# Weights laid out by tiles, and the decode's gate sums taken for all samples in one product

## The chip, the core and the metric

The kernel runs on one core of one Trainium2 chip. The metric is the device time of one execution in microseconds (us), and lower is better. The kernel is built by hand from single instructions for the engines of the core: TensorE (PE, matrix products, with a separate record for its weight loads, PEld), VectorE (DVE), ScalarE (ACT), GpSimd (POOL) and SyncE (SP). SP, POOL and ACT also issue DMAs, and each of them has a queue of its own for that: the profile calls SP's queue q1, ACT's q10 and POOL's q0.

## What is computed

One inference step of a one-layer decoder in float32. A prompt of 1024 rows and 8 samples of one row each share the weights. Per layer:

```python
q, k, v, logf, u, z = mixer_inputs(rmsnorm(x), w_in, b_f, g_sgu_v)      # x @ w_in, columns split
...
c = cumsum(lf_all, axis=1)                  # forget gates, past positions from the paged cache, then the new one
s = q @ k_all.T * 64 ** -0.5 + (c[query] - c[key])
att = softmax(s) @ v_all                    # 8 heads of 64; a sample has 8192 past positions in 64 pages
x = x + concat(rmsnorm(att), rmsnorm(sgu(u, z))) @ w_o
x = x + cross_attend(rmsnorm(x), memory keys and values from w_ck, w_cv, with w_cq, w_co)
x = x + (silu(conv(gate)) * conv(val)) @ w_down      # h = rmsnorm(x) @ w_up
```

A sample's keys, values and gate logs are gathered from three caches through a page table: 16 gathers of 1 MB for the keys of a sample (4 positions by 512 numbers for each of 128 partitions), 16 for the values, and one of 256 KB for the gate logs (64 positions by 8 heads for each partition). A position's gate is the sum of all gate logs behind it. On the chip this is a scan inside each partition's 64 positions, and a product with a constant matrix of suffix sums, `suf`, over the 128 partitions' totals.

## The kernel before

The prompt sets the program: the input projection in the order of its columns q (O_Q), forget and u (O_F, 520 columns), k (O_K), v (O_V), z (O_Z), then attention in two halves, the output projection, cross attention and the MLP. Every float32 product is made of three products of split operands: a weight is loaded raw into `wr` (L249), ACT rounds it to `wh` (L235), DVE takes the rest `wl = wr - wh` (L236), and PE multiplies three times (L272 wh by u, L273 wl by u, L274 wh by the rest of u). So no product of L273 can start before DVE has made the `wl` of its pair of row blocks. `wr` and `wl` have 4 buffers each, `wh` 5, so that the splits of a stage also wait for the products of the stage before. A load brings 512 KB (256 rows by 512 columns), issued by SP in program order, so that all of SP's transfers stand in one line in q1. `wpair` (L264) gives the address of such a load.

Beside the prompt runs the decode of the 8 samples, as a background program that is stepped between pieces of the prompt's work (L1525 and on). For sample b it takes 16 steps ch: a gather of keys (POOL, L1428), a product with the query on DVE (L1444, or L1435 in attention) and a sum over the 64 numbers of each head (L1448 or L1436). The query is fetched by SP through a copy in memory (L1398). At ch 11 `gates_scan` gathers the gate logs (L1404), reorders them on ACT (L1407) and scans them on DVE (L1408). At ch 13 `gates` adds the 64th value of the scan to the new row's gate (L1413), multiplies with `suf` on PE (L1418, into the PSUM bank "ms", of which there is one, shared with the attention's products) and subtracts the scan on DVE (L1420), which gives `dec`. Then the values are gathered (L1489) and multiplied on PE (L1495).

All order is fixed when the program is built: each engine runs its rows in the order in which they were written, with `behind(...)` and `issue_after(...)` moving rows to a place behind what has been written on that engine, and waits only on semaphores. The names below: `kv` is a buffer of gathered keys or values (4 of them), `d` a buffer of 128x512 (5 of them, for queries, gate logs and scans), `s` a sample's scores, `lps` the sums of its exponentials, `fl` the prompt's forget logits, `lse` and `lf` the steps of their log sigmoid (L364 to L367).

Of the kernel before, what the change touches and what calls it, by code (L numbers as in the profile page):

```python
# [11 lines left out]
AF = mybir.ActivationFunctionType  # L12
ALU = mybir.AluOpType
# [5 lines left out]
P = 128  # L19
# [59 lines left out]
def build(nc, tc, ctx, a, phases=None):  # L79
# [27 lines left out]
    def nm(s):  # L107
        cnt[0] += 1
        return f"{s}_{cnt[0]}"
# [245 lines left out]
    lfz = const.tile([P, 64], F32, tag="lfz", name="lfz")  # L355
    lps = const.tile([P, 8, 8], F32, tag="lps", name="lps")
    dec = lambda tag: dpool.tile([P, 512], F32, tag=tag, bufs=1, name=nm(tag))
    vsum = dec("vsum").rearrange("p (b d) -> p b d", d=64)
# [15 lines left out]
    def p1(early):  # L374
# [13 lines left out]
        def load_x(kk, hf):  # L388

            raw = WRAW(1024).rearrange("p (k t) -> p k t", t=512)  # L390
            c = slice(hf * 512, hf * 512 + 512)
# [291 lines left out]
    def pmem():  # L683
# [9 lines left out]
        for q in range(2):  # L693
            h, l = U([P, 4, 256], F32R), U([P, 4, 256], F32R)
            raw = WRAW(1024).rearrange("p (k m) -> p k m", m=256)
            nc.sync.dma_start(raw, a["memT"][q * 512 : (q + 1) * 512, :].rearrange("(k p) m -> p k m", p=P))
            for k in range(4):
# [440 lines left out]
    def cross(xt, sq):  # L1138
# [84 lines left out]
        for n in range(2):  # L1223
            if n:
                ws = [wload(wpair(a["w_cq"], kk, n * 512, 512), 1024) for kk in range(4)]
            for dt_ in range(4):
# [35 lines left out]
        ys = []  # L1262
        sq = yield from out_proj(a["w_co"], oh, ol, xt, ys=ys)
        return ys
# [4 lines left out]
    def ffn(hf, xt, ys, late=None):  # L1269
# [21 lines left out]
        for gi, gn in enumerate(GROUPS):  # L1291
# [32 lines left out]
            for n in range(2):  # L1324
                ws = []
                for k2 in range(0, gn, 2):
                    m = min(2, gn - k2)
                    r0 = (f0 + k2) * P
                    h, l, _ = wload(
                        a["w_down"][r0 : r0 + m * P, n * 512 : (n + 1) * 512].rearrange("(k p) n -> p k n", p=P), m * 512  # L1330
                    )
                    for q in range(m):
                        ws.append((h[:, q, :], l[:, q, :]))
# [40 lines left out]
    def decode():  # L1374
# [35 lines left out]

        def gates(b, A):
            tot = sm([P, 8], "tot", 2)
            nc.vector.tensor_tensor(  # L1413
                tot, A.rearrange("p (h k) -> p h k", k=64)[:, :, 63], lfz[:, b * 8 : b * 8 + 8], op=ALU.add
            )
            ps = MS()
            with behind(ENG.PE):
                mmul(ps[:, :8], suf, tot, start=True, stop=True)  # L1418
            dt_ = dec("dec").rearrange("p (k h) -> p k h", h=8)
            nc.vector.tensor_tensor(  # L1420
                dt_, ps[:, :8].unsqueeze(1).broadcast_to((P, 64, 8)), A.rearrange("p (h k) -> p k h", k=64), op=ALU.subtract
            )
            return dt_
# [103 lines left out]
        for g in range(8 * 16 + 16 + VLAG + 2):  # L1527
# [326 lines left out]
    def prompt():  # L1854
# [38 lines left out]
        for hf in range(2):  # L1893
# [8 lines left out]
            if ends:  # L1902
                yield from ends.pop()
            sq = yield from out_proj(a["w_o"], mh, ml, xt, partial(load_x, hf))
            if hf == 0:
# [43 lines left out]
    "cpack", "gpack", "b_f", "g_sgu_v", "ws00", "bs00", "wsT", "w_in", "w_o", "w_cq", "w_ck", "w_cv", "w_co",  # L1949
    "w_up", "w_down", "g_final",  # L1950
]
# [6 lines left out]
def layout(np, i):  # L1958
# [15 lines left out]
    for m in range(2):  # L1974
# [8 lines left out]
        axis=1,  # L1983
    )
    x = n["x_prompt"][0]
    xs = n["x_sample"][:, 0]
    return {
        "x": f(x), "xT": f(x.T), "xs": f(xs), "xsT": f(xs.T.reshape(8, P, 8).transpose(1, 0, 2)),
        "cache_k": f(n["cache_k"]).reshape(-1, 4 * AW), "cache_v": f(n["cache_v"]).reshape(-1, 4 * AW),
        "cache_logf": f(n["cache_logf"]).reshape(-1, 64 * NH),  # L1990
        "cmk": f(n["cache_mem_k"][0]).reshape(NB, NMEM, D), "cmv": f(n["cache_mem_v"][0]).reshape(NB, NMEM, D),
        "stT": f(n["state_conv"][0].transpose(2, 1, 0).reshape(2 * NF, P, 16).transpose(1, 0, 2)),
        "pt": f(n["page_table"].T), "mem": f(n["mem_prompt"][0]), "memT": f(n["mem_prompt"][0].T),
        "cpack": cp, "gpack": f(gp), "b_f": f(n["b_f"]), "g_sgu_v": f(n["g_sgu_v"]),
        "ws00": f(n["w_s"][0][:, 0, 0][None]), "bs00": f(n["b_s"][0][:, 0][None]),
        "wsT": f(n["w_s"][0].transpose(2, 0, 1)),
        "w_in": f(n["w_in"][0]), "w_o": f(n["w_o"][0]), "w_cq": f(n["w_cq"][0]), "w_ck": f(n["w_ck"][0]),
        "w_cv": f(n["w_cv"][0]), "w_co": f(n["w_co"][0]),
        "w_up": f(n["w_up"][0].reshape(8, P, 2 * NF, P).transpose(2, 1, 0, 3)).reshape(2 * NF, P, D),
        "w_down": f(n["w_down"][0]), "g_final": f(n["g_final"][None]),  # L2000
    }
# [33 lines left out]
```

## Time and profile before

| what | before |
|---|---|
| time of three runs, us | 1790.99, 1791.04, 1794.76 (median 1791.04) |
| span of the profiled execution, us | 1791.7 |
| DVE busy, us | 1399.9 (78%) in 1733 instructions |
| ACT busy, us | 733.5 (41%) |
| POOL busy, us | 488.3 (27%) |
| DMA moved | 521.06 MB in 157074 packets |
| of it on q1 (SP) | 165.73 MB in 92874 packets |
| of it on q0 (POOL) | 341.14 MB in 57168 packets |

The profile has one execution, whose span is 1791.7 us; this is 0.7 us above the median of the runs. An engine's busy time against the span says how much it could still wait. Where the span is set by one engine, the rows to read are its idle times and what ended them; the rest of the table tells what the other engines may be late with.

### The profile page before, as it was taken

Reading aid. Unit: us, or ns where it says so; the run is one execution under the profiler, and the core shown is the slowest. Engines: PE = TensorE matmul, PEld = TensorE weight load, DVE = VectorE, ACT = ScalarE, POOL = GpSimd, SP = SyncE. Lnnn points to the kernel's source line nnn. Section 1 sums busy time; section 2 is a strip of 40 time slices with the busy share of each in tenths; the row PEclk is TensorE's granted clock in tenths of the full one; section 3 lists DMA queues with packets and bytes.
Section 4 is the critical chain, followed back from the end, with each engine's and each line's share of the span. In section 5 each row is a group of like instructions: output and inputs, shape, how many; then the busy total and the mean of one; then the engine's idle time right before and its main releaser. Section 6 shows DMA issues by size and latency. Waiting matters only on the chain.

```text
span 1791.7 us, 25124 instructions
## 1 busy us (share of the span) xinstructions
PE 1735.9 (97%) x9653; PEld 1285.7 (72%) x9653; DVE 1399.9 (78%) x1733; ACT 733.5 (41%) x1374; POOL 488.3 (27%) x461
## 2 busy tenths in 40 slices
PE   8999999889999999999999999999999999999997
PEld 5787777655677666767777777766666778768875
DVE  4689658989788986989999999898885549855344
ACT  6332355566643635333333244335353233333232
POOL 1252234443222332333322223433322112102110
PEclk9999999999999999999999999999999999999999
DMA  8786798777697975779788788988879587568982
GB/s 291 297 304 226 294 334 319 259 264 244 254 403 279 363 299 224 282 285 345 290 301 313 291 317 311 376 306 346 320 280 350 214 306 249 191 260 297 359 310 80
DMA packets 157074, 521.06 MB, mean 291 GB/s; under 512 B 20874, under 2 KB 40842, under 8 KB 124186
## 3 DMA queue, kind: packets, MB, share of 16 engines
q0 software_dynamic: 57168, 341.14, 50.0%
q1 hardware_dynamic: 92874, 165.73, 26.5%
q10 hardware_dynamic: 6912, 12.59, 1.9%
q8 instruction: 76, 1.25, 0.3%
q14 instruction: 44, 0.36, 0.1%
HBM read 495.47 MB, written 23.93 MB: 290 GB/s over the span
## 4 chain that ended last, share of the span: by engine, by line
PE 53%; issue 9%; DMA 8%; DVE 6%; ACT 2%; POOL 2%; POOLq 0%; DVEq 0%; ACTq 0%; SPq 0%
DMA kv<-cache_v,io 6%; PE ba L272 6%; PE ba L274 6%; PE ba L273 6%; PE dv L1495 4%; PE bb L272 3%; PE bb L273 3%; PE bb L274 3%; PE ba L1063 1%; DVE s L1448 1%; PE ba L1064 1%; PE ba L1065 1%; PE dv L331 1%; DMA kv<-cache_k,io 1%; PE dv L1774 1%
## 5 line engine op out<-in xcount | busy, mean ns | idle before, releaser
L235 ACT ACTIVATE wh<-wr 128x1024 fp32r<-128x1024 f32 (+2 forms) x220 | 228.6, 1044 | 443.3 <-PE ba L273 142.3
L236 DVE TENSOR_TENSOR wl<-wr,wh 128x1024 fp32r<-128x1024 f32 (+2 forms) x220 | 262.7, 1200 | 165.1 <-PE ba L274 57.4
L1428 POOL DMA_INDIRECT kv<-cache_k,io x128 | 186.9, 1460 | 606.8 <-DVE s L1448 327.2
L1444 DVE TENSOR_TENSOR kv<-kv,d 128x1024 f32<-128x1024 f32 (+1 forms) x156 | 258.0, 1681 | 32.6 <-DMA kv<-cache_k,io 32.6
L1448 DVE TENSOR_REDUCE s<-kv 128x16 f32<-128x1024 f32 (+1 forms) x156 | 258.4, 1672 | 0.0
L1489 POOL DMA_INDIRECT kv<-cache_v,io x128 | 160.8, 1256 | 239.4 <-PE dv L1495 155.2
L272 PE MATMUL ba<-u,wh 128*128 128x512 f32 x528 | 209.3, 397 | 0.0
L274 PE MATMUL ba<-u,wl 128*128 128x512 f32 x528 | 209.0, 396 | 0.0
L273 PE MATMUL ba<-u,wh 128*128 128x512 f32 x528 | 208.5, 395 | 0.5 <-DVE u L239 0.5
L272 PE MATMUL ba<-wh,u 128*128 128x512 f32 (+1 forms) x495 | 186.1, 379 | 0.9 <-ACT u L235 0.9
L273 PE MATMUL ba<-wl,u 128*128 128x512 f32 (+1 forms) x495 | 185.1, 375 | 1.3 <-DVE wl L236 1.3
L274 PE MATMUL ba<-wh,u 128*128 128x512 f32 (+1 forms) x495 | 183.4, 375 | 0.0
L1495 PE MATMUL dv<-kv,s 128*32 128x512 f32 x1024 | 127.1, 598 | 1.6 <-DMA kv<-cache_v,io 1.6
L274 PEld LDWEIGHTS ba<-u,wl 128*128 128x128 f32 x528 | 99.2, 188 | 29.0 <-issue 6.5
L272 PEld LDWEIGHTS ba<-u,wh 128*128 128x128 f32 x528 | 99.3, 188 | 26.4 <-issue 4.8
L273 PEld LDWEIGHTS ba<-u,wh 128*128 128x128 f32 x528 | 99.2, 188 | 25.2 <-issue 2.3
L272 PEld LDWEIGHTS ba<-wh,u 128*128 128x128 f32 x495 | 93.0, 188 | 25.0 <-issue 6.5
L272 PE MATMUL bb<-u,wh 128*128 128x512 f32 x272 | 108.7, 400 | 0.0
L274 PE MATMUL bb<-u,wl 128*128 128x512 f32 x272 | 108.0, 398 | 0.0
L273 PE MATMUL bb<-u,wh 128*128 128x512 f32 x272 | 107.9, 397 | 0.0
L273 PEld LDWEIGHTS ba<-wl,u 128*128 128x128 f32 x495 | 93.0, 188 | 20.1 <-DVE wl L236 1.9
L274 PEld LDWEIGHTS ba<-wh,u 128*128 128x128 f32 x495 | 92.9, 188 | 19.5 <-issue 1.6
(454 smaller groups left out, 3310.6 us busy)
## 6 DMA issues: line engine op xcount, KB each, us to landing
wr<-w_up SPq DMA_DIRECT2D x88, 512.0 KB
kv<-w_up POOLq DMA_DIRECT2D x22, 1024.0 KB
wr<-w_down SPq DMA_DIRECT2D x40, 512.0 KB
kv<-w_down POOLq DMA_DIRECT2D x11, 1024.0 KB
wr<-w_in SPq DMA_DIRECT2D x16, 512.0 KB
wr<-w_o SPq DMA_DIRECT2D x16, 512.0 KB
wr<-w_cq SPq DMA_DIRECT2D x16, 512.0 KB
wr<-w_co SPq DMA_DIRECT2D x16, 512.0 KB
```

What stands on the lines that cost most here:

```text
L235: nc.scalar.activation(h, src, AF.Copy)
L236: nc.vector.tensor_tensor(l, src, h.bitcast(F32), op=ALU.subtract)
L272: mmul(out, sh, mh, start=(i == 0), stop=False)
L273: mmul(out, sh, ml, start=False, stop=False)
L274: mmul(out, sl, mh, start=False, stop=(i == n - 1))
L331: mmul(ps[32 * j : 32 * j + 32, :w], xT[:, k, :] if nk == 8 else xT[:, k * 8 : k * 8 + 32], raw[:, q, j * w : (j + 1) * w], start=(k == 0) ...
L1063: mmul(pss[i], mh[k][:, tb], wh, start=(k == korder[0]), stop=False)
L1428: nc.gpsimd.indirect_dma_start(kv, None, a["cache_k"], off(kidx[:, b, ch : ch + 1]))
L1444: nc.vector.tensor_tensor(kvv[:, i : i + m, :], kvv[:, i : i + m, :], qb.unsqueeze(1).broadcast_to((P, m, 512)), op=ALU.mult)
L1448: nc.vector.tensor_reduce(s[:, ch * 4 + i : ch * 4 + i + m, :].rearrange("p k h -> p (k h)"), kvv[:, i : i + m, :].rearrange("p k (h d) -> ...
L1489: nc.gpsimd.indirect_dma_start(kv, None, a["cache_v"], off(kidx[:, b, ch : ch + 1]))
L1495: mmul(dv[32 * j : 32 * j + 32, :], s[:, ch * 4 : ch * 4 + 4, :].rearrange("p k h -> p (k h)"), kvv[:, j, :], start=(ch == 1), stop=(ch == ...
```

## The change

Two things are changed. First, the inputs `xT`, `memT`, `w_in`, `w_ck` and `w_cv` are stored "by tiles": for each of a weight's column groups, the 128 rows of a block go to the partitions, and a partition's numbers of successive blocks lie one behind the other. A load of two blocks by 512 columns, which read 256 runs of 2 KB, reads 128 runs of 4 KB (for O_F 128 of 4160 bytes in place of 256 of 2080; for `memT` 4 KB in place of 1 KB). `w_o`, `w_cq`, `w_co` and `w_down` are handed over a second time in this form (`wt_o`, `wt_cq`, `wt_co`, `wt_down`), for the prompt; the decode's projections read the plain ones. `w_up` had runs of 4 KB before.

Second, the totals of all 8 samples' gate logs are made in steps 2 to 9 of sample 0: a second gather of each sample's gate logs and a sum over the 64 positions. In step 12 of sample 0 the 128x64 totals and the new rows' gates are added, one product with `suf` is made, and ACT copies it back to `lfz`. `gates` then only subtracts the scan from it.

```diff
     def wpair(w, kk, c0, n):
-        return w[kk * 256 : (kk + 1) * 256, c0 : c0 + n].rearrange("(k p) n -> p k n", p=P)
+        return w[:, 8 * c0 + kk * 2 * n : 8 * c0 + (kk + 1) * 2 * n].rearrange("p (k n) -> p k n", n=n)
...
-            nc.sync.dma_start(raw, a["xT"][kk * 256 : (kk + 1) * 256, c].rearrange("(k p) t -> p k t", p=P))
+            nc.sync.dma_start(raw, wpair(a["xT"], kk, hf * 512, 512))
...
-        ws = [wload(wpair(a["w_cq"], kk, 0, 512), 1024) for kk in range(4)]
+        ws = [wload(wpair(a["wt_cq"], kk, 0, 512), 1024) for kk in range(4)]
...
-        def gates(b, A):
-            tot = sm([P, 8], "tot", 2)
-            nc.vector.tensor_tensor(
-                tot, A.rearrange("p (h k) -> p h k", k=64)[:, :, 63], lfz[:, b * 8 : b * 8 + 8], op=ALU.add
-            )
+        def total(b):
+            lg = D2()
+            nc.gpsimd.indirect_dma_start(lg, None, a["cache_logf"], off(lidx[:, b : b + 1]))
+            with behind(ENG.DVE):
+                nc.vector.tensor_reduce(tots[:, b, :], lg.rearrange("p (k h) -> p h k", h=8), axis=AX.X, op=ALU.add)
+        def suffixes():
+            nc.vector.tensor_tensor(lfz, lfz, tots.rearrange("p b h -> p (b h)"), op=ALU.add)
             ps = MS()
             with behind(ENG.PE):
-                mmul(ps[:, :8], suf, tot, start=True, stop=True)
+                mmul(ps[:, :64], suf, lfz, start=True, stop=True)
+            nc.scalar.activation(lfz, ps[:, :64], AF.Copy)
+        def gates(b, A):
             dt_ = dec("dec").rearrange("p (k h) -> p k h", h=8)
             nc.vector.tensor_tensor(
-                dt_, ps[:, :8].unsqueeze(1).broadcast_to((P, 64, 8)), A.rearrange("p (h k) -> p k h", k=64), op=ALU.subtract
+                dt_, lfz[:, b * 8 : b * 8 + 8].unsqueeze(1).broadcast_to((P, 64, 8)), A.rearrange("p (h k) -> p k h", k=64), op=ALU.subtract
             )
...
                 left = yield from kstep(b, ch, st[b])
+                if b == 0 and 2 <= ch < 10:
+                    total(ch - 2)
+                if b == 0 and ch == 12:
+                    suffixes()
```

The totals lie in the same tile as `lps` (`tots = lps`), which is free until sample 0's exponentials. The line numbers behind the change are 6 higher in the decode's steps (L1444 is L1450, L1448 is L1454, L1404 and L1408 are L1402 and L1406).

The first place where rows move is DVE in the input projection, at the first four key products of sample 0 in the O_F stage. Before, these rows stand there (`fl` is the prompt's forget logit, the scan is that of sample 0's gate logs):

```order
L1444 TENSOR_TENSOR kv_485<-kv_485,d_61_345 128x2048
L513 SCALAR_TENSOR_TENSOR fl_596<-ba_597,rstd,bfb 128x8
L1408 SCALAR_TENSOR_TENSOR d_133_1077<-rmask,d_133_1077 128x512
L1448 TENSOR_REDUCE s_347<-kv_348 128x32
L1448 TENSOR_REDUCE s_347<-kv_388 128x32
L1448 TENSOR_REDUCE s_347<-kv_453 128x32
L1448 TENSOR_REDUCE s_347<-kv_485 128x32
```

With the change the same place on DVE reads as follows (the rows of L1414 are the new totals, written into the tile `lps`):

```order
L1450 TENSOR_TENSOR kv_488<-kv_488,d_61_345 128x2048
L513 SCALAR_TENSOR_TENSOR fl_605<-ba_606,rstd,bfb 128x8
L1414 TENSOR_REDUCE lps<-d_71_457 128x8
L1414 TENSOR_REDUCE lps<-d_75_492 128x8
L1454 TENSOR_REDUCE s_347<-kv_348 128x32
L1414 TENSOR_REDUCE lps<-d_79_527 128x8
L1414 TENSOR_REDUCE lps<-d_106_669 128x8
L1454 TENSOR_REDUCE s_347<-kv_388 128x32
```

Four of the eight totals now stand between the key products and the key sums; the scan has moved behind them.

The second place is DVE at the end of that stage, where the first `wl` of O_K is made. Before:

```order
L1444 TENSOR_TENSOR kv_839<-kv_839,d_61_345 128x2048
L1448 TENSOR_REDUCE s_347<-kv_780 128x32
L513 SCALAR_TENSOR_TENSOR fl_596<-ba_957,rstd,bfb 128x8
L1444 TENSOR_TENSOR kv_953<-kv_953,d_61_345 128x2048
L1448 TENSOR_REDUCE s_347<-kv_839 128x32
L513 SCALAR_TENSOR_TENSOR fl_596<-bb_1016,rstd,bfb 128x8
L236 TENSOR_TENSOR wl_1098<-wr_1096,wh_1099 128x1024
```

With the change:

```order
L1450 TENSOR_TENSOR kv_857<-kv_857,d_61_345 128x2048
L1454 TENSOR_REDUCE s_347<-kv_795 128x32
L1406 SCALAR_TENSOR_TENSOR d_398_2490<-rmask,d_398_2490 128x512
L1450 TENSOR_TENSOR kv_974<-kv_974,d_61_345 128x2048
L513 SCALAR_TENSOR_TENSOR fl_605<-bb_1040,rstd,bfb 128x8
L236 TENSOR_TENSOR wl_1122<-wr_1120,wh_1123 128x1024
```

The key sum that belongs to the last but one gather (`kv_839` before, `kv_857` now) stood ahead of this `wl` and now stands behind it; the four other totals and the two scans stand ahead of it, between the rows of the place before and this one. At the first `wl` of O_V it is the other way round: of the key sums one more stands ahead of it than before.

The third place is PE in the first half of attention, at the gates of sample 1. Before (`ms` is the shared bank, `bb` and `ba` are other banks, `t` and `u` tiles of the attention):

```order
L807 MATMUL ba_2752<-u_2331,u_2327 128x384
L809 MATMUL ba_2752<-u_2331,u_2327 128x384
L811 LDWEIGHTS ident_b
L811 MATMUL ba_2752<-cmask_b,ident_b 128x128
L1418 MATMUL ms_2720<-tot_2718,cp 128x8
L836 MATMUL bb_2759<-cp,t_444_2671 128x128 x2
L852 MATMUL ms_2790<-t_413_2553,u_2302 64x256
L852 MATMUL ms_2790<-t_440_2658,u_2302 64x256
```

With the change:

```order
L807 MATMUL ba_2772<-u_2355,u_2351 128x384
L809 MATMUL ba_2772<-u_2355,u_2351 128x384
L811 LDWEIGHTS ident_b
L811 MATMUL ba_2772<-cmask_b,ident_b 128x128
L852 MATMUL ms_2810<-t_420_2577,u_2326 64x256
L836 MATMUL bb_2779<-cp,t_451_2695 128x128 x2
L852 MATMUL ms_2810<-t_447_2682,u_2326 64x256
```

The gate product of sample 1 is gone from PE, and the attention's own product into the bank "ms" follows at once; `dec` of sample 1 is made far ahead, on DVE in the O_V stage.

More of the change, by code (lines that the diff above doesn't have):

```diff
@@ L1262, in cross @@
         ys = []
[L1263 removed]
+        sq = yield from out_proj(a["wt_co"], oh, ol, xt, ys=ys)
         return ys
@@ L1996, in layout @@
         "wsT": f(n["w_s"][0].transpose(2, 0, 1)),
-        "w_in": f(n["w_in"][0]), "w_o": f(n["w_o"][0]), "w_cq": f(n["w_cq"][0]), "w_ck": f(n["w_ck"][0]),
-        "w_cv": f(n["w_cv"][0]), "w_co": f(n["w_co"][0]),
+        "w_in": tiles(n["w_in"][0], [(O_Q, 512), (O_K, 512), (O_V, 512), (O_F, 520), (O_Z, 512)]),
+        "w_o": f(n["w_o"][0]), "w_cq": f(n["w_cq"][0]), "w_ck": tiles(n["w_ck"][0], halves),
+        "w_cv": tiles(n["w_cv"][0], halves), "w_co": f(n["w_co"][0]),
         "w_up": f(n["w_up"][0].reshape(8, P, 2 * NF, P).transpose(2, 1, 0, 3)).reshape(2 * NF, P, D),
+        "wt_o": tiles(n["w_o"][0], halves), "wt_cq": tiles(n["w_cq"][0], halves), "wt_co": tiles(n["w_co"][0], halves),
+        "wt_down": tiles(n["w_down"][0], halves),
         "w_down": f(n["w_down"][0]), "g_final": f(n["g_final"][None]),
```

24 lines of the change are left out of this document (13 added, 11 removed).

## The prediction

> **What bounds the kernel now.** I read the page's first part, then the waits of PE, then the timeline of PE at each wait.
>
> ```profile
> span 1791.7 us, 25124 instructions
> PE 1735.9 (97%) x9653; PEld 1285.7 (72%) x9653; DVE 1399.9 (78%) x1733; ACT 733.5 (41%) x1374; POOL 488.3 (27%) x461
> ```
>
> PE is busy for 1735.9 of 1791.7 us. So a change can save PE's own work or some of the 55.8 us in which PE stands still, and nothing else. A faster transfer counts only where PE waits behind it. The waits of PE say where that could be (engine, bank and line, what it waited for: us in total, times, longest):
>
> ```profile
> PE ba L306 <- DVE u L239: 7.1, 1, 7.1
> ...
> PE ms L852 <- DVE dec L1420: 2.7, 1, 2.7
> ...
> PE bb L836 <- ACT t L843: 1.7, 1, 1.7
> ...
> PE dv L1495 <- DMA kv<-cache_v,io: 1.6, 2, 1.3
> ...
> PE bb L306 <- DMA wr<-w_in: 1.6, 2, 1.2
> PE ms L852 <- DVE t L841: 1.4, 1, 1.4
> ...
> PE ba L273 <- DVE wl L236: 1.3, 3, 0.7
> ```
>
> Row 1 is the start. Rows 2, 5 and 7 belong to the two halves of this change: the wait for `dec` hangs on the gate product in the bank "ms", the waits for `w_in` and its `wl` hang on late weights. All weights together, 166 MB of them, hold PE up in one place only, and that place is the input projection.
>
> **The layout.** Three queues share the 16 DMA engines. The DMA view of 42 to 44 us (gathers of keys on q0 against `w_in` of O_F on q1; packets, MB, share of the engines' time) and that of 29 to 40 us (loads in runs of 4 KB alone) price a packet:
>
> ```profile
> q0 software_dynamic: 84, 0.64, 77.1%
> q1 hardware_dynamic: 89, 0.17, 22.9%
> ...
> q1 hardware_dynamic: 1168, 4.33, 100.4%
> ```
>
> 84 packets against 89: the queues take turns packet by packet. A gather's packet takes 0.771 x 32 / 84 = 0.294 us (16 engines, 2 us), one of 2080 bytes 0.229 x 32 / 89 = 0.082 us, one of 4 KB 1.004 x 176 / 1168 = 0.151 us. A pair of turns brings 2080 bytes of weights in 0.376 us now and 4160 in 0.445 then: under contention the same load takes 0.59 of the time. [...]
>
> Where PE waits for it (timeline of PE in O_F; start, us, in brackets the idle time before and its releaser):
>
> ```profile
> 58.96 1.05 PE L306 MATMUL bb<-wr,xg 128*32 128x512 f32 x4 [0.43 <-DMA wr<-w_in]
> ...
> 61.23 1.05 PE L306 MATMUL bb<-wr,xg 128*32 128x512 f32 x4 [1.17 <-DMA wr<-w_in]
> ...
> 64.09 0.39 PE L273 MATMUL ba<-wl,u 128*128 128x260 f32 x1 [0.72 <-DVE wl L236]
> ...
> 65.24 0.39 PE L273 MATMUL ba<-wl,u 128*128 128x260 f32 x1 [0.17 <-DVE wl L236]
> ...
> 66.58 0.39 PE L273 MATMUL ba<-wl,u 128*128 128x260 f32 x1 [0.35 <-DVE wl L236]
> ```
>
> The idle times add up to 2.84 us. The loads of O_F follow the x loads at about 40 and the last lands at 61.2; 0.59 of these 21 us is 12.5, so it lands at about 52.5, ahead of PE's need. All 2.84 us go. The start (7.1 us, of which only the transfer of 512 KB shrinks) I put at -0.2, bounds 0 and -0.7.
>
> **What the totals do to DVE.** The saving must pass DVE, which in the next 50 us has no gap (timeline of DVE, then its groups from 63 to 128 us and over the whole run, then PE's last product of O_Q and its first of O_K that needs a `wl`):
>
> ```profile
> 53.19 1.24 DVE L236 TENSOR_TENSOR wl<-wr,wh 128x1040 fp32r<-128x1040 f32 x1 [7.73 <-PE ba L273]
> 62.79 3.74 DVE L236 TENSOR_TENSOR wl<-wr,wh 128x1040 fp32r<-128x1040 f32 x3 [8.36 <-ACT wh L235]
> 66.45 8.89 DVE L1444 TENSOR_TENSOR kv<-kv,d 128x2048 f32<-128x2048 f32 x4
> ...
> 111.63 1.20 DVE L236 TENSOR_TENSOR wl<-wr,wh 128x1024 fp32r<-128x1024 f32 x1
> ```
>
> ```profile
> L1448 DVE TENSOR_REDUCE s<-kv 128x32 f32<-128x2048 f32 x12 | 27.0, 2268 | 0.0
> ```
>
> ```profile
> L1485 DVE TENSOR_REDUCE lps<-s 128x8 f32<-128x512 f32 x8 | 8.9, 1115 | 0.0
> ```
>
> ```profile
> 57.09 0.40 PE L274 MATMUL ba<-wh,u 128*128 128x512 f32 x1
> ...
> 115.78 0.39 PE L273 MATMUL bb<-wl,u 128*128 128x512 f32 x1
> ```
>
> A total has the form of L1485, a sum over 64 positions read with a stride: 1.1 us, some 1.05 of it in a dense stream, so 8 x 1.05 = 8.4 us more ahead of the first `wl` of O_K, less the one L1448 (2.27) that moves behind it: +6.1. Against this stands how much sooner DVE begins. Its first split of O_F waited for PE (53.19), the next for ACT and so for the late load (62.79). With the loads early, each of the four waits only for PE to finish with the buffer of one block of O_Q, (57.09 - 53.19) / 3 = 1.3 us apart, and DVE is through at about 59 in place of 66.45. I take 7 us sooner; bounds 0 and 8.4. Then the first `wl` is ready at 111.63 + 1.20 + 6.1 - 7 = 111.9, and PE wants it at 115.78 - 2.84 - 0.2 = 112.7: no wait, with 0.8 us to spare. **Each us below 6.3 sooner is a us of waiting at O_K.**
>
> At O_V one more key sum stands ahead of the first `wl`:
>
> ```profile
> 133.70 0.15 DVE L367 SCALAR_TENSOR_TENSOR lfs<-fs,lse 8x8 f32<-8x8 f32 x1 [5.47 <-ACT lse L366]
> ...
> 162.75 1.21 DVE L236 TENSOR_TENSOR wl<-wr,wh 128x1024 fp32r<-128x1024 f32 x1
> ```
>
> ```profile
> 165.01 0.40 PE L273 MATMUL ba<-wl,u 128*128 128x512 f32 x1
> ```
>
> Between these two rows DVE runs without a gap. Its wait of 5.47 us ends with ACT, which evicts PE's products of O_K; it follows PE. Three small rows now stand ahead of it, and on ACT one more eviction. I put the end of that wait 2.5 us sooner. The `wl` is then ready at 163.96 - 2.5 + 2.27 - 0.1 = 163.6, PE wants it at 162.0: 1.6 us of waiting. Left of the 3.0 us are **1.4**. Bounds: -3.0 (no wait at O_V) and +7.4 (rival B).
>
> The eight added gathers (2 MB) cost 1 us of POOL each (its group, then its timeline behind the first key gathers):
>
> ```profile
> L1404 POOL DMA_INDIRECT d<-cache_logf,lidx x8 | 7.7, 962 | 2.3 <-issue 2.0 <-ACT u L1234 0.3
> ```
>
> ```profile
> 79.05 0.95 POOL L1428 DMA_INDIRECT kv<-cache_k,io  x1 [28.18 <-DVE s L1448]
> ```
>
> The first ones go out behind the first four key gathers, where POOL next waits 28 us for a key buffer; the rest wait for a total to free a buffer `d`, in the order in which the key sums free theirs. They are hidden by the DVE stream, which reads them 10 us later. If that cover failed, one transfer of 256 KB, some 1 us, would show.
>
> **What the gates free.** PE's gate product among other work, for a later sample:
>
> ```profile
> 1006.51 0.28 PE L1418 MATMUL ms<-tot,cp 128*128 128x8 f32 x2
> 1006.65 0.48 PE L274 MATMUL ba<-wh,u 128*128 128x512 f32 x1
> 1006.97 0.40 PE L274 MATMUL bb<-wh,u 128*128 128x512 f32 x1
> ```
>
> 0.14 us to the next start and 0.32 to the one after, where 0.23 is the pitch: 0.23 us. Seven fewer: **1.6** (bounds 1.0 and 2.0). For sample 1 it also costs a wait (PE, DVE, ACT, then the windows of 3.41 us with busy times of PE, PEld, DVE, ACT, POOL and the granted clock):
>
> ```profile
> 314.39 0.34 PE L1418 MATMUL ms<-tot,cp 128*128 128x8 f32 x2
> ...
> 317.72 1.12 PE L852 MATMUL ms<-t,u 128*64 128x256 f32 x4 [2.72 <-DVE dec L1420]
> ```
>
> ```profile
> 316.64 1.02 DVE L1420 TENSOR_TENSOR dec<-ms,d 128x512 f32<-128x512 f32 x1
> ```
>
> ```profile
> 315.59 0.38 ACT L843 ACTIVATE t<-bb 128x256 f32<-128x256 f32 x1
> ```
>
> ```profile
> 317.28:320.69 3.41, 2.97 (x16) 2.26 (x16) 3.32 (x6) 0.64 (x3) 0.60 (x2) 0.50 1.05 407
> ```
>
> PE's product into "ms" waits until DVE, behind a split and a maximum, has read the gate product. With the change the bank is free. Late next is ACT, whose copy ends at 315.97: PE has 4 products of its own until about then, so 1.7 of 2.72 us go (bounds 0.6 and 2.72). The wait is also followed by a stretch of 3.41 us at half clock (0.50), with PE busy 2.97; a wait of 1 us should not bring that. At most half of the 2.97 is lost there; I take **1.0** (bounds 0 and 1.5). Together 2.7.
>
> The other loads (w_o, w_cq, w_co, w_down, w_ck, w_cv) save nothing, since PE does not wait for them. They take more of a turn from the gathers of values: a gather has 8 packets of 8 KB on each engine, so a pair in flight can land 16 x (0.151 - 0.082) = 1.1 us later. PE waited for values twice (1.6 us): 0 to +2.2, taken at 0, since only two of some 64 pairs are on the edge.
>
> The sum: -1.4 - 1.6 - 2.7 = **-5.7** against 1791.7, or 1786.0. The median of the runs lies 0.7 lower, which gives 1785.3. All rows behind sample 0 shift a little, and PE's other waits (1.7 for L836, 1.4 for L852) may come or go; I take 0, bounds -3 and +3, and name **1785.8**, half a us toward the time before, since the O_V term leans on the longest chain.
>
> **Rivals.** (A) The queue's share does not grow, or the loads are late for another reason. Then PE keeps its 2.84 us in O_F, DVE starts no sooner, the first `wl` of O_K is ready at 112.83 + 6.1 = 118.9 against 115.78 (+3.2), and at O_V one more key sum less the slack there, 2.2 - (165.01 - 163.96) = 1.1, comes on top: +4.3 - 1.6 - 2.7 = 0, 1791 us. For it: I know turns only from one window of 2 us. Against: both kinds of packet have their prices there.
>
> (B) Slower, by the totals on DVE. The loads are early, but DVE isn't: the split waits for PE's buffers or the key product for its query, and the 5.47 us at 133.70, a wait for ACT, moves along with DVE and takes up nothing. All 8.4 us then reach O_V: 162.75 + 1.21 + 8.4 = 172.4 against 165.0, +7.4, and two waits of over 3 us bring half clock, 1.0 each. +9.4 - 1.6 - 2.7 = +5.1: 1796 us. It decides from there: DVE starts less than 6.3 us sooner and has no real gap before O_V. For it: no gap from 63 to 128 us. Against, the row of DVE's busy time from O_K to O_V, 43.79 of 50.20 us:
>
> ```profile
> 112.80:163.00 50.20, 50.12 (x235) 37.54 (x228) 43.79 (x41) 17.74 (x25) 16.10 (x8) 1.00 0.70 236
> ```
>
> (C) More. DVE is in time at O_V too (-3.0), the wait at 314 goes whole (-2.7, clock -1.5), the gates give 1.6 and the two waits in attention 3.1 go with the new order: -11.9, 1779 us, and about 1782 with half of the extra.
>
> **Chances.** The forecast 0.45, A 0.22, B 0.14, C 0.19. A measurement of this kernel tells about 0.2%, 3.6 us, from no change: faster means below 1787.4, slower above 1794.6. Of the forecast's 0.45, 0.38 lie below 1787.4; with C that makes faster 0.57. Same: 0.07, A's 0.20 and 0.01 of B, 0.28. Slower: 0.15. The range 1779.5 to 1795 leaves out the ends of B and C.
>
> **What would show it.** Layout: q1's share beside gathers near a third in place of 22.9%, no wait of L306 for `w_in`. DVE: the splits of O_F done by 60, no wait of L273 for `wl` at O_K and one of 1 to 2 us at O_V; waits of 3 us at either mean A or B. Gates: one L1418 in place of eight, no wait for `dec` at 314 and full clock behind it. I am wrong if DVE is not free before 60, or if new waits in attention, where the order of all rows shifts, are larger than the 2.7 us removed.

## The result, and the profile after

The changed kernel takes 1813.3 us (median of 5 runs, 1810.3 to 1819.7) against 1791.0 (5 runs of the kernel before on the same chip, 1788.5 to 1794.8): ratio **1.0122, 95% interval 1.0099 to 1.0145**, 22 us slower. The prediction said 1785.8. The profiled execution has a span of 1817.6 us.

The first part of its page, then PE's waits:

```profile
span 1817.6 us, 25123 instructions
PE 1740.6 (96%) x9639; PEld 1288.6 (71%) x9639; DVE 1406.1 (77%) x1734; ACT 731.9 (40%) x1375; POOL 507.7 (28%) x469
```

```profile
PE dv L1501 <- DMA kv<-cache_v,io: 14.0, 4, 7.4
PE ba L306 <- DMA wr<-w_in: 7.4, 1, 7.4
PE ba L273 <- DVE wl L236: 6.8, 1, 6.8
PE bb L1188 <- ACT t L1175: 4.3, 1, 4.3
...
PE bb L273 <- DVE wl L236: 3.4, 1, 3.4
```

PE stands still for 77.0 us in place of 55.8, and is busy 4.7 us longer with 14 products fewer: some of its work ran at half clock (0.51 and 0.50 in the two windows below). The row of 7.4 us for `w_in` is the start of the program, which was 7.1 us before (there put down to `u`). The waits that were to go did go (`w_in` in O_F, `dec` at 314). New are the two for `wl`, 10.2 us, and 12.4 us more for gathered values; the 4.3 us at L1188 lie in cross attention. POOL's busy time rose by 19.4 us; eight gathers more at 0.97 us explain 7.7.

When each part was lost is seen by pairing the rows of ACT and DVE of two traces (the n-th row of a source line and form with the n-th) and taking, in stretches of 10 us, the median of how much later than before they start. The columns are places of the program, by the time they have in the kernel before; the kernels below the first are the experiments, one profiled execution each. Executions of one kernel differ (the runs of e12 go from 1786.6 to 1809.1 us), so a loss that one trace shows need not be in each of them.

| kernel, us later than before at | 70 | 120 | 190 | 240 | 560 | 640 | 1150 | 1330 |
|---|---|---|---|---|---|---|---|---|
| after | -3.9 | 4.6 | 9.1 | 11.8 | 11.5 | 18.2 | 17.3 | 24.1 |
| e1_layout | -4.2 | -2.5 | -4.1 | -4.1 | -5.9 | -4.9 | -2.1 | -3.0 |
| e3_short_totals | -4.2 | 1.9 | -3.2 | -0.5 | -2.7 | 3.4 | 2.1 | 9.6 |
| e13_after_psum | -3.9 | 4.6 | 1.8 | 4.4 | 2.6 | 10.1 | 10.5 | 12.7 |
| e15_short_psum | -2.8 | 0.1 | -4.3 | -1.6 | -1.6 | 8.1 | 5.6 | 7.6 |
| e6_totals_beside | -3.9 | 4.6 | 1.9 | 4.5 | 9.1 | 14.0 | 15.3 | 17.4 |
| e7_copy | -4.0 | -2.4 | 1.6 | 1.6 | 3.5 | 11.5 | 13.6 | 17.9 |
| e12_copy_unused | -3.6 | -3.6 | -3.6 | -3.6 | 2.0 | 8.4 | 10.0 | 8.3 |
| e13b_later_psum | -3.9 | -4.3 | -1.4 | -3.7 | -2.5 | 3.2 | 2.3 | 7.2 |

The changed kernel gains 4 us by 70, loses 15.7 until 240 (stages O_K and O_V), 6.7 between 560 and 640 (cross attention), and 6.8 between 1150 and 1330.

### The profile page after: what moved, and what is told of

It reads as the page before. It is cut to its first block, busy times and chain, and to the rows that moved or that the text cites. A ratio compares the mean times of both kernels' runs of the same rounds, so it can differ in the third digit from the quotient of the medians.

```text
span 1817.6 us, 25123 instructions
## 1 busy us (share of the span) xinstructions
PE 1740.6 (96%) x9639; PEld 1288.6 (71%) x9639; DVE 1406.1 (77%) x1734; ACT 731.9 (40%) x1375; POOL 507.7 (28%) x469
## 4 chain that ended last, share of the span: by engine, by line
PE 54%; issue 6%; DMA 6%; DVE 4%; POOL 2%; ACT 1%; POOLq 0%; DVEq 0%
PE ba L274 8%; PE ba L272 8%; PE ba L273 8%; PE dv L1501 5%; PE bb L272 4%; PE bb L274 4%; PE bb L273 4%; DMA kv<-cache_v,io 2%; DMA kv<-w_up 2%; DVE kv L1450 1%; DMA kv<-cache_k,io 1%; PE ba L1065 1%; PE ba L1064 1%; PE ba L1063 1%; PE ba L1081 1%
## 5 line engine op out<-in xcount | busy, mean ns | idle before, releaser
L1450 DVE TENSOR_TENSOR kv<-kv,d 128x1024 f32<-128x1024 f32 (+1 forms) x156 | 257.8, 1680 | 33.8 <-DMA kv<-cache_k,io 32.9
L1454 DVE TENSOR_REDUCE s<-kv 128x16 f32<-128x1024 f32 (+1 forms) x156 | 258.4, 1673 | 0.0
L1495 POOL DMA_INDIRECT kv<-cache_v,io x128 | 173.2, 1353 | 253.6 <-PE dv L1501 178.6
```

The lines of the kernel that those rows point to most:

```text
L1450: nc.vector.tensor_tensor(kvv[:, i : i + m, :], kvv[:, i : i + m, :], qb.unsqueeze(1).broadcast_to((P, m, 512)), op=ALU.mult)
L1454: nc.vector.tensor_reduce(s[:, ch * 4 + i : ch * 4 + i + m, :].rearrange("p k h -> p (k h)"), kvv[:, i : i + m, :].rearrange("p k (h d) -> ...
L1495: nc.gpsimd.indirect_dma_start(kv, None, a["cache_v"], off(kidx[:, b, ch : ch + 1]))
```

## Where O_K and O_V lose 15.7 us

DVE from the splits of O_F on (timeline of after), then ACT at the same place:

```profile
54.10 1.24 DVE L236 TENSOR_TENSOR wl<-wr,wh 128x1040 fp32r<-128x1040 f32 x1 [9.40 <-issue]
57.97 3.74 DVE L236 TENSOR_TENSOR wl<-wr,wh 128x1040 fp32r<-128x1040 f32 x3 [2.62 <-ACT wh L235]
62.52 8.90 DVE L1450 TENSOR_TENSOR kv<-kv,d 128x2048 f32<-128x2048 f32 x4 [0.81 <-DMA d<-qs_d]
...
114.02 3.47 DVE L236 TENSOR_TENSOR wl<-wr,wh 128x1024 fp32r<-128x1024 f32 x3
...
168.44 2.29 DVE L1450 TENSOR_TENSOR kv<-kv,d 128x2048 f32<-128x2048 f32 x1 [3.52 <-DMA kv<-cache_k,io]
...
172.84 2.35 DVE L236 TENSOR_TENSOR wl<-wr,wh 128x1024 fp32r<-128x1024 f32 x2
```

```profile
56.87 2.04 ACT L235 ACTIVATE wh<-wr 128x1040 fp32r<-128x1040 f32 x2 [3.72 <-PE ba L273]
```

The key products start at 62.52 in place of 66.45: 3.9 us sooner, not 7. The loads were early, but the second split of O_F waited on ACT (2.62 us), and ACT for PE to free a buffer of `wh` (3.72 us); the query came 0.8 us later still. The totals cost what was forecast (eight, 1139 ns the median one), so the first `wl` of O_K comes 2.4 us later than before while PE comes sooner. At O_V it starts 10.1 us later than before (172.84 against 162.75), of which 3.5 are a wait for a gather of keys. PE, and two windows around the waits (busy times of PE, PEld, DVE, ACT, POOL, then the granted clock):

```profile
115.28 0.79 PE L273 MATMUL bb<-wl,u 128*128 128x512 f32 x1 [3.35 <-DVE wl L236]
...
174.11 0.80 PE L273 MATMUL ba<-wl,u 128*128 128x512 f32 x1 [6.76 <-DVE wl L236]
```

```profile
114.00:120.90 6.90, 5.62 (x13) 4.45 (x14) 6.90 (x7) 0.43 (x1) 1.72 (x2) 0.51 0.80 294
172.10:178.90 6.80, 4.79 (x11) 3.80 (x12) 6.80 (x6) 0.96 (x1) 2.93 (x2) 0.50 0.55 193
```

With each wait come some 6.8 us at half clock (0.51 and 0.50), which begin 1.3 and 2.0 us before PE goes on. If half of PE's busy time in them is lost (an estimate), 10.1 us of waits and (5.62 + 4.79) / 2 = 5.2 of clock make 15.3 of the 15.7.

The gather behind the 3.5 us is held by POOL itself (timeline of POOL, after):

```profile
154.07 9.48 POOL L1434 DMA_INDIRECT kv<-cache_k,io  x1 [1.24 <-DVE cc L537]
163.56 0.59 POOL L759 DMA_DIRECT2D u<-cq_d  x1
165.19 1.02 POOL L1434 DMA_INDIRECT kv<-cache_k,io  x1 [1.04 <-DVE s L1454]
```

A gather takes about 1 us of POOL (the median is 0.96); this one takes 9.48. Beside it DVE makes `dec`, whose two operands are both in SBUF now, and three key products, and POOL comes free in the key sum behind them. Such holds are not new: the kernel before has one of 6.30 us at 111.84, beside splits and a key product. So there were two theories for O_V: the totals (rival B), and a subtraction that no longer reads PSUM.

## The experiments

Every kernel keeps the layout unless told otherwise. A changed row also changes what the program's own ordering makes of DVE and POOL, so each edit moves some rows besides; a theory O, that any new order costs, had to be excluded too. Each ratio is against runs of the kernel before that were taken with the experiment; their median lies between 1789.6 and 1794.1 us, so times of different experiments are compared by their ratios.

**The two halves.** Layout alone, with the gates of before, and gates alone, with the layout of before:

```diff
 e1_layout: wpair, tiles and the wt_ weights as in the change; gates(b, A) as before, no total, no suffixes
 e2_gates:  total, suffixes and gates(b, A) as in the change; wpair and the inputs as before
```

> The layout alone, with the gates of before; the order of rows on every engine is that of before. Theory L (the larger turns of the weights push back the gathers of values): the 2.8 us of O_F are saved, but the waits of PE for cache_v stay at about 14 us as in the changed kernel, with some 3 us at half clock: about 1803 us. Theory T (the loss comes from the totals on DVE in the input projection, and later losses from the new order of rows): no wait at O_K and O_V, waits for cache_v at 1 to 3 us: 1787 to 1789 us.

> The gates alone, with the layout of before; the order of rows is that of the changed kernel. Theory T: the splits of O_F are late as before, so the first wl of O_K is ready at about 119 and PE waits there 3 us and at O_V 6 us or more; with half clock and the O_F stalls the input projection loses 12 to 15 us, and the later waits (cache_v, L1188) are there too: 1812 to 1818 us. Theory L: only the input projection loses, waits for cache_v stay at 1 to 3 us: 1800 to 1804 us.

Measured: layout 1791.6 us, ratio 0.9999 [0.9984, 1.0013]; gates 1815.9, 1.0131 [1.0112, 1.0150]. The whole loss comes from the gates. The layout does to the input projection what was forecast and pays nothing that the runs can tell, though its profiled execution is 3 us shorter.

**The totals.** The sum over 1 of 64 positions, and the other way round the eight gathers and totals beside the gates of before, read by nobody:

```diff
 e3_short_totals against the changed kernel
-  nc.vector.tensor_reduce(tots[:, b, :], lg.rearrange("p (k h) -> p h k", h=8), axis=AX.X, op=ALU.add)
+  nc.vector.tensor_reduce(tots[:, b, :], lg.rearrange("p (k h) -> p h k", h=8)[:, :, 0:1], axis=AX.X, op=ALU.add)
 e6_totals_beside against e1_layout
+  if b == 0 and 2 <= ch < 10:
+      total(ch - 2)
```

> The changed kernel with each total summed over 1 of the 64 positions only (the other 63 are left out), so that a total takes some 0.1 us of DVE in place of 1.1; the rows of the input projection move a little, the order behind it is the same. Theory T for the input projection: no wait for wl at O_K, at most 2 us at O_V, full clock, the 11.5 us lost up to 200 us go: about 1802 us, with the waits for cache_v left. If the key gathers and not the sums were what DVE is late with, it stays above 1808 us.

> The new layout and the gates of before, with the eight gathers and sums of totals added in steps 2 to 9 of sample 0 and not used. Theory T: these sums on DVE are the whole loss of the input projection, whatever is done with them: waits of PE for wl of 3 us at O_K and 5 to 7 at O_V, half clock behind both, 11 us more than the layout alone, 1802 us. Theory O (the other half of the loss is the new order of the rows behind it): the order behind the input projection is nearly that of before here, so not much is added to these 11 us: 1801 to 1806. Against both: 1813, which would put the later loss on the totals too.

Measured: short totals 1801.9 us, 1.0044 [1.0025, 1.0063]; totals alone 1805.5, 1.0059 [1.0039, 1.0079]. With short totals the waits for `wl` fall to 0.6 us, and about two thirds of the loss are gone; the waits for values stay (PE's waits, e3):

```profile
PE dv L1501 <- DMA kv<-cache_v,io: 12.0, 4, 5.8
PE ba L306 <- DMA wr<-w_in: 7.6, 1, 7.6
PE bb L1188 <- ACT t L1175: 3.5, 1, 3.5
```

The two thirds are not the totals' alone. In e3 the subtraction of O_V stands behind the three key products (155.14) and no longer ahead of them, and the gather at 147.54 takes 1.22 us. The totals alone (e6) bring waits for `wl` of 3.9 us at O_K and 2.6 at O_V, where 5 to 7 had been expected, and make the kernel 8.6 us later at 240 than the layout alone. From 280 to 300 e6 loses 6.4 us more, which was not expected: ACT waits 3.3 us for a load of `w_cv`, and PE 3.57 for ACT. e12 below has the same (3.23 and 3.48 us). The changed kernel doesn't.

**The layout behind the input projection.**

```diff
 e4_after_inproj against the changed kernel
-  ws = [wload(wpair(a["wt_cq"], kk, 0, 512), 1024) for kk in range(4)]
+  ws = [wload(rpair(a["w_cq"], kk, 0, 512), 1024) for kk in range(4)]
   (so too w_ck, w_cv, w_o, w_co, w_down, memT; xT and w_in stay by tiles)
```

> The changed kernel with the new layout for xT and w_in only; memT, w_ck, w_cv, w_o, w_cq, w_co and w_down are read in runs of before; order of rows as in the changed kernel. Theory L: the waits for cache_v fall from 14 to about 2 us with their half clock: 1796 to 1800 us. Theory T with the new order: they stay, 1811 to 1815 us.

Measured: 1813.1 us, 1.0113 [1.0096, 1.0131]; the new layout matters neither way behind the input projection, and the waits for values (10.4 us here) are not its doing.

**The operand of the subtraction.** First as the change has it, without totals; then the same with the copy read by nobody:

```diff
 e7_copy against e1_layout
+  sx = lfz[:, b * 8 : b * 8 + 8]
+  nc.scalar.activation(sx, ps[:, :8], AF.Copy)
-  dt_, ps[:, :8].unsqueeze(1)...
+  dt_, sx.unsqueeze(1)...
 e12_copy_unused against e7_copy
-  dt_, sx.unsqueeze(1)...
+  dt_, ps[:, :8].unsqueeze(1)...
```

> The new layout and the gates of before, one product for each sample, but ACT copies its result out of the bank ms at once and the subtraction reads the copy; no totals. If the bank was what cost 2.7 us and the half clock behind it, 3 to 4 us go: 1787 to 1789 us. If moving rows is a risk in itself (theory O), the time may rise by some us here too although nothing is added: 1794 to 1800.

> As e7 (layout, ACT copies the gate product out of the bank "ms" into SBUF for every sample), but the subtraction reads the bank as before; the copy is read by nobody. This takes the operand of the subtraction apart from the added ACT row. Theory P (a subtraction with two operands in SBUF keeps GpSimd from issuing gathers, one with an operand in PSUM does not): the gather of keys at about 147 us takes 1 to 4 us, not 9.5; PE waits for cache_v under 4 us in all (8.6 in e7); ratio 0.999 to 1.003. Rival Q (the copy itself, its wait and the rows that the program's scheduler moved because of it): the gather and the cache_v waits stay as in e7 and the ratio stays at 1.006 to 1.010.

Measured: e7 1810.5 us, 1.0080 [1.0057, 1.0104], above all that had been expected of it; e12 1797.5, 1.0016 [0.9992, 1.0039]. The same gather in both (POOL, then DVE beside it), e7 first:

```profile
147.04 9.49 POOL L1427 DMA_INDIRECT kv<-cache_k,io  x1 [1.25 <-DVE cc L536]
...
147.70 1.08 DVE L1419 TENSOR_TENSOR dec<-lfz,d 128x512 f32<-128x512 f32 x1
148.71 0.41 DVE L544 TENSOR_SCALAR t<-t 8x512 f32<-8x512 f32 x1
149.04 6.67 DVE L1443 TENSOR_TENSOR kv<-kv,d 128x2048 f32<-128x2048 f32 x3
155.65 2.27 DVE L1447 TENSOR_REDUCE s<-kv 128x32 f32<-128x2048 f32 x1
161.58 2.29 DVE L1443 TENSOR_TENSOR kv<-kv,d 128x2048 f32<-128x2048 f32 x1 [3.67 <-DMA kv<-cache_k,io]
```

```profile
146.38 1.21 POOL L1427 DMA_INDIRECT kv<-cache_k,io  x1 [1.25 <-DVE cc L536]
...
147.03 1.06 DVE L1419 TENSOR_TENSOR dec<-ms,d 128x512 f32<-128x512 f32 x1
148.02 0.41 DVE L544 TENSOR_SCALAR t<-t 8x512 f32<-8x512 f32 x1
148.36 6.68 DVE L1443 TENSOR_TENSOR kv<-kv,d 128x2048 f32<-128x2048 f32 x3
154.96 2.27 DVE L1447 TENSOR_REDUCE s<-kv 128x32 f32<-128x2048 f32 x1
157.16 2.27 DVE L1443 TENSOR_TENSOR kv<-kv,d 128x2048 f32<-128x2048 f32 x1
```

The DVE rows are the same, and the gather begins 0.66 and 0.65 us ahead of `dec`. In these rows only its operand differs: from "ms" it lets POOL through in 1.21 us, from `lfz` in SBUF POOL is held until the sum at 155.65, and the key product of that gather waits 3.67 us. PE then waits 4.2 us for `wl` at O_V in e7 and not at all in e12. The copy does not do this. e12 falls into the range of theory P in all three points (PE's waits for values are 1.4 us).

**The operand put back in the changed kernel**, with whole totals and with short ones:

```diff
 e13_after_psum against the changed kernel (e15_short_psum: and the short totals of e3)
+  ps = MS()
+  nc.scalar.activation(ps[:, :8], lfz[:, b * 8 : b * 8 + 8], AF.Copy)
-  dt_, lfz[:, b * 8 : b * 8 + 8].unsqueeze(1)...
+  dt_, ps[:, :8].unsqueeze(1)...
```

> The changed kernel, but ACT copies the sample's 8 sums back into the bank ms and the subtraction reads them there, as before, and only the scan from SBUF. Theory P (with both operands in SBUF the subtraction closes the gaps in which POOL issues gathers between the products of DVE; a gather that needed 1.2 us in the layout alone needed 9.5 us at the same place): no gather of more than 5 us in the O_V stage, no wait of DVE for cache_k there, the waits of PE for cache_v at 1 to 3 us in place of 14; the wait at O_K from the totals stays: 1798 to 1804 us. If the totals and the new order were all: 1811 to 1816.

> The kernel after with both parts taken away: the totals run over 1 of 64 positions (63 are left out, the gates are not those of the reference), and the subtraction reads PSUM (ACT copies the sample's 8 sums back into "ms"). Theory S (the totals on DVE and the operand are the whole loss): no wait for wl at O_K and O_V above 1 us, no 9.5-us gather, and a time within 3 us of before: ratio 0.998 to 1.002. Rival R (a third part, in cross attention and the steps behind it, comes with any such move of rows): on time until about 560 us, then 5 to 10 us lost between 560 and 660 or at 1200 to 1300: ratio 1.004 to 1.007.

Measured: e13 1808.0 us, 1.0111 [1.0087, 1.0134]; e15 1801.3, 1.0032 [1.0013, 1.0051]. In e13 the long gather of O_V is gone, the wait for `wl` there falls from 6.76 to 1.77 us, and one wait for values is left (2.9 us); by 240 us it is 7.4 us ahead of the changed kernel. In its runs as a whole that gain isn't to be told from nothing, and the 1808.0 us lie between what theory P and its rival gave. e15 is ahead of before at 240 and at 560, then loses 9.7 us by 640. Its ratio lies between what theories S and R gave, and the place is R's: there is a third part.

**The third part, in cross attention.** The same rows in e1, which loses 1 us there, and in e12, which loses 6.4 (POOL, DVE, PE; the last row of each is the same products of PE):

```profile
598.63 1.68 POOL L1425 DMA_INDIRECT kv<-cache_k,io  x1 [1.67 <-DVE s L1445]
...
598.29 2.35 DVE L1441 TENSOR_TENSOR kv<-kv,d 128x1024 f32<-128x1024 f32 x2
600.55 2.35 DVE L236 TENSOR_TENSOR wl<-wr,wh 128x1024 fp32r<-128x1024 f32 x2
602.83 1.21 DVE L1445 TENSOR_REDUCE s<-kv 128x16 f32<-128x1024 f32 x1
...
613.36 3.72 PE L1187 MATMUL ba<-t,u 128*128 128x256 f32 x16 [0.93 <-ACT t L1174]
```

```profile
606.52 5.08 POOL L1427 DMA_INDIRECT kv<-cache_k,io  x1 [1.67 <-DVE s L1447]
...
606.16 2.36 DVE L1443 TENSOR_TENSOR kv<-kv,d 128x1024 f32<-128x1024 f32 x2
608.43 2.36 DVE L236 TENSOR_TENSOR wl<-wr,wh 128x1024 fp32r<-128x1024 f32 x2
610.70 1.22 DVE L1447 TENSOR_REDUCE s<-kv 128x16 f32<-128x1024 f32 x1
...
619.10 2.36 DVE L1443 TENSOR_TENSOR kv<-kv,d 128x1024 f32<-128x1024 f32 x2 [3.18 <-DMA kv<-cache_k,io]
...
624.14 6.70 PE L1187 MATMUL ba<-t,u 128*128 128x256 f32 x16 [3.83 <-ACT t L1174]
```

In e12 this gather is held through two key products and two splits, all with two operands in SBUF, until the sum at 610.70. The keys are 3.18 us late, a maximum of the attention stands behind them on DVE, PE waits 3.83 us and then runs its products in 6.70 us in place of 3.72; the granted clock is 0.67 over 620 to 630 us, where e1 has 1.00 in each 10 us from 560 to 650. e15 has the same with a gather of 6.28 us at 607.07, and besides it a wait of 5.00 us at 609.64, as the reciprocal of the softmax's sums now stands on DVE behind a split and two key sums. So the third part consists of the second mechanism at another place and of an order that is worse there. What the runs don't settle is why the gather of e1 came through between the two key products and that of e12, 0.36 us into the same rows in place of 0.34, did not. The changed kernel has a gather of 5.09 us at 621.45 there, but its wait of 4.26 us at L1188 ends at 622.6, 1.1 us after that gather began, and ACT, for which PE waits there, had been busy without a gap since 615.5: this wait is not the hold's doing.

**Is any new order dearer?** The gates one step earlier (rows move about as much as in the change) and one later, with the work of e1:

```diff
 e9_gates_ch12 (and e9_gates_ch14 with 14) against e1_layout
-  if ch == 13:
+  if ch == 12:
```

> The new layout and the gates of before, called in step 12 in place of step 13: not one instruction more or less, only other places of rows (about as many rows of PE and DVE stand elsewhere as between before and the changed kernel; the products of values near 1200 to 1300 us stand up to 46 products of the prompt later). Theory O: a new order alone costs, mostly in the two stretches of cross attention (560 to 630 and 1200 to 1300 us), with waits of PE for cache_v and for L1175: 1797 to 1810 us. Against theory O: within 3 us of the layout alone.

> The new layout and the gates of before, called in step 14 in place of step 13: again no instruction more or less, but here the order is close to that of before (POOL the same but for two rows, the products of values within 3 products of their places). Theory O: close to the layout alone, 1788 to 1795 us; a loss of 8 us or more here would say that even such a small shift decides.

Measured: 1793.6 us, 1.0016 [0.9999, 1.0032], and 1792.9, 0.9995 [0.9979, 1.0011]. Theory O falls as a general cause: these two moved the order and cost at most some 0.3%. But e9_gates_ch12, in which no gather there takes more than 1.7 us, shows what an order alone can do in cross attention (PE's waits; this one ends at 601.0 us, and the trace makes it up elsewhere):

```profile
PE bb L1187 <- ACT t L1174: 3.4, 1, 3.4
```

**Keeping the one product at a lower price.** Sample 0 as before, the totals of samples 1 to 7 made during sample 1 (e8); the same with the subtraction from "ms" (e13b); the same with the subtraction on ACT (e14):

```diff
 e8_totals_later against e1_layout
+  if b == 1 and 2 <= ch < 9:
+      total(ch - 1)
+  if b == 1 and ch == 12:
+      suffixes()
 e14_later_act against e8_totals_later
-  nc.vector.tensor_tensor(dt_, lfz[...].broadcast_to((P, 64, 8)), A..., op=ALU.subtract)
+  for h in range(8):
+      nc.scalar.activation(dt_[:, :, h], A[:, h * 64 : h * 64 + 64], AF.Identity, scale=-1.0, bias=lfz[:, b * 8 + h : b * 8 + h + 1])
```

> The new layout; sample 0's gates as before, the totals of samples 1 to 7 in steps 2 to 8 of sample 1, behind the input projection, one product for the seven. The order of rows behind the input projection is nearly that of the changed kernel. Theory T alone: no wait for wl in the input projection, no wait at 314, all of the loss gone: 1786 to 1789 us. Theory T with O: the 11 us of the input projection go, and the waits for cache_v and L1188 stay: 1798 to 1804 us.

> The run with the totals of samples 1 to 7 in sample 1, and the subtraction reading from the bank ms as before through a copy by ACT. Theory P with T: neither the totals nor closed gaps: 4 to 9 us less than with the subtraction from SBUF, 1789 to 1794 us where the kernel before has 1791 to 1794. Without P: as that run, 0.2% above the kernel before.

> The run with the totals of samples 1 to 7 in sample 1, and the subtraction of samples 1 to 7 made by ACT in 8 pieces (bias from SBUF), so that DVE has 7 us less to do and POOL is not shut out by it. Theory P: at or below the kernel before, 1785 to 1792 us, with waits of PE for cache_v at 1 to 3 us. If ACT, which feeds PE in cross attention, is late by the 8 pieces: waits of PE for ACT t L1175 of 4 us and more, 1795 to 1802.

Measured: e8 1798.8 us, 1.0019 [1.0002, 1.0036]; e13b 1800.6, 1.0056 [1.0040, 1.0072]; e14 1791.2, 1.0005 [0.9992, 1.0018]. e8 has no wait for `wl` above 0.4 us in the input projection, and most of the loss back. Taking its operand back to PSUM did not help it (e13b), against theory P, which had given 1789 to 1794: 15.9 us of waits for values fell to 5.0, and the runs became no shorter. e14, in its trace, was up to 11 us ahead of before until 1170 and lost it by 1350, with waits at L1188 (7.1 us in all, for ACT), the risk that had been named for it. None of the versions beats the kernel before.

## Why the prediction was wrong

**The layout: right, and worth nothing in the end.** The DMA view of 42 to 44 us now reads

```profile
q0 software_dynamic: 76, 0.53, 63.8%
q1 hardware_dynamic: 83, 0.29, 36.1%
```

83 packets against 76: the queues still take turns, and q1's share grew from 22.9% to 36.1%, near the third that was named as the sign. PE's waits for `w_in` in O_F are gone, and 3.9 us were gained by 70 us where 3.0 were forecast. Rival A falls. But e1 as a whole is at 0.9999 of before.

**The first step that failed, DVE's start.** "I take 7 us sooner; bounds 0 and 8.4": it was 3.9, since the working left out that ACT, ahead of DVE, waits for PE to free a buffer (3.72 us), and DVE then for the query (0.8). The splits of O_F were done at 61.7, so the sign "I am wrong if DVE is not free before 60" came true. Its own rule then gives the result: 2.4 us short of 6.3, and PE there 0.8 us sooner than was worked out (115.28 - 3.35 = 111.9 in place of 112.7), make 3.2 us of waiting at O_K; 3.35 were measured. The price of a total, 1.05 to 1.1 us, was right (1.14).

**O_V: rival B, and more.** The forecast was 1.6 us of waiting; rival B, given a chance of 0.14, had 7.4 with two half-clock stretches. Measured were 6.76. Rival B's condition held: DVE started less than 6.3 us sooner, and found no gap that would take up the totals (its wait of 5.47 us became one of 2.81 at 138.21, but one of 2.60 at 142.28 came with it). B had nothing on the held gather, whose 3.5 us stand in the 10.1 by which this `wl` is late, so that its 7.4 came near 6.76 in part by luck. Its clock term, 1.0 for each wait, was too small, as each wait came with 6.8 us at half clock and cost some 2.6 (the same estimate).

**The second step that failed** is the sentence "All rows behind sample 0 shift a little, and PE's other waits ... may come or go; I take 0, bounds -3 and +3". Nothing in the working asked what it does to POOL that `dec` now reads SBUF twice. e7 against e12 prices that edit, alone, at 0.6% (1.0080 against 1.0016), some 11 us. Beside the whole totals it shows by 240 us (e13: 7.4 us). It shows again near 1260: the five kernels that read SBUF there in the order of the change (after, e2, e3, e4 and e8) all have a gather of values held for 6.3 to 7.0 us and a wait of PE for values of 5.5 to 7.4; e6, e12, e13, e13b and e15, which read PSUM, have none above 1.2. From 1150 to 1330 the changed kernel loses 6.8 us and e3 7.5; e1, e6, e12, e13 and e15 between -1.7 and 2.2. The operand isn't the only way to lose there: e13b, which reads PSUM, loses 4.9, with waits at L284 and L1188, and e7's loss stands at another wait (3.95 us at L1187, for ACT). In the changed kernel (POOL, DVE, PE):

```profile
1252.15 7.04 POOL L1495 DMA_INDIRECT kv<-cache_v,io  x1 [0.93 <-PE dv L1501]
1259.50 4.29 POOL L1495 DMA_INDIRECT kv<-cache_v,io  x1 [0.30 <-issue]
...
1253.90 2.37 DVE L1450 TENSOR_TENSOR kv<-kv,d 128x1024 f32<-128x1024 f32 x2
1256.17 1.07 DVE L1426 TENSOR_TENSOR dec<-lfz,d 128x512 f32<-128x512 f32 x1
1257.15 1.23 DVE L236 TENSOR_TENSOR wl<-wr,wh 128x1024 fp32r<-128x1024 f32 x1
...
1271.07 3.64 PE L1501 MATMUL dv<-kv,s 128*32 128x512 f32 x16 [7.44 <-DMA kv<-cache_v,io]
```

The prediction saw a risk of late values only in the new layout (0 to +2.2, taken at 0); in e1 they are 2.4 us, 0.8 more than before, so that term was within its bounds.

**The gates: the wait went, the gain did not show.** No product waits for `dec` at 314, and, as forecast, the copy on ACT is late next, with a wait of 0.5 us:

```profile
327.74 0.86 PE L852 MATMUL ms<-t,u 128*64 128x256 f32 x6 [0.53 <-ACT t L843]
...
342.27 0.55 PE L836 MATMUL bb<-cp,t 128*128 128x128 f32 x3 [1.62 <-ACT t L814]
```

Yet the changed kernel is as late at 420 (11.0) as at 300 (11.7), while e13, which has the wait for `dec` back (2.5 us), catches up 2.9 there. So the 2.7 and the 1.6 us of seven products saved were not separable from the other waits of attention, and were not measured by themselves. That a wait of 1 us should not bring half clock was the author's estimate, and the traces show both cases: in the kernel before, PE goes on behind the wait of 1.17 us at 61.23 with a clock of 1.00 (61.23 to 66 us), and behind one of 1.08 us at 354.00 it has 3.41 us at 0.50 from 354.8 on; the changed kernel has 3.41 us at 0.50 from 342.7 on, behind the 1.62 us above.

**The sum.** Of 22 us between the medians, e15, without long totals and without the operand in SBUF, has 0.9 of 1.2% back; what is left it loses, in its trace, in cross attention. Up to 240 us the two causes nearly add up: against the layout alone the totals (e6) cost 8.6 us and the operand (e7) 5.7, together 14.3, where the whole change costs 15.9. In whole runs they add up only one way. Added to the layout, they cost 0.6% (e6) and 0.6% (e7 against e12). Taken out of the change, short totals bring 0.8% back, with an order that also spares the gather of O_V, and the operand (e13) 0.1%, not told from nothing. What each kernel loses besides in attention and cross attention depends on its order, and the runs do not settle it.

## What to carry to other kernels

Before an operand is moved from PSUM to SBUF, ask which transfers GpSimd issues beside the instruction that reads it. Here a subtraction from SBUF and three key products behind it (6.67 us, two operands in SBUF each) held such an issue for 9.49 us, into the next key sum, and the cost appeared further on as late data: 3.67 us on VectorE, and 4.2 us on TensorE for `wl` (e7). Work added to an engine in a stretch without gaps is late for the first product behind it by all that an earlier start does not cover (2.4 us at O_K); so a start that is to be earlier has to be followed through every engine in between, here ACT's wait of 3.72 us for a buffer. The two waits of PE cost more than themselves, since 6.9 and 6.8 us at a clock of 0.51 and 0.50 came with the 3.35 and the 6.76 us, some 2.6 us more each by the estimate above.

## What the hardware showed that was not expected

GpSimd's indirect gather took 1.21 us beside a VectorE subtraction with one operand in PSUM (e12), and 9.49 us beside the same rows with both operands in SBUF (e7), of which 3.67 us reached VectorE itself as late keys. The trace has one row for the whole gather, so the runs do not show what in it is held up. The blocked gather outlasted the subtraction, three products and the 0.41-us row of one operand between them, so that gap was not enough to let it in. In e12 the gather ended at 147.59, during the subtraction from PSUM (1.06 us from 147.03 on), ahead of the first product at 148.36. The subtraction is not needed for a hold: in e13b, where it reads PSUM, a gather of gate logs that begins with the first of four key products (145.86) takes 9.71 us, though DVE and PE do not wait for it, and the 6.30 us at 111.84 in the kernel before have splits and a key product beside them and no subtraction. Why some gathers come through between two products and others don't, the runs leave open.
